# First feed-forward of a hybrid attention and recurrence step: a ring of its own for kept weight tiles, loaded one ahead

## Chip, cores and metric

One Trainium2 chip, one core. The metric is the device time of the kernel in microseconds: the median of three runs before the change is 1487.94 us (1484.69, 1487.94 and 1488.04). One further execution was profiled; every row below is from that one.

## What is computed

Two layers of a denoising step on 640 tokens (512 latent, 128 context) of width 1024. Layer 0 is attention, layer 1 a gated linear recurrence, and each is followed by a SwiGLU feed-forward of inner width 2816. Every sub-layer is normalised, scaled and shifted by columns that come from a small "adaLN" product, and added back through a gate. Cut to what the change touches:

```python
def _adaln(cond, w_mod, b_mod):
    m = jax.nn.silu(cond) @ w_mod + b_mod
    return jnp.split(m, N_MOD, axis=-1)

def _swiglu(x, w_gu, w_down):
    gate, up = jnp.split(x @ w_gu, 2, axis=-1)
    return (jax.nn.silu(gate) * up) @ w_down

# in the loop over the two layers
        f_c = _swiglu(_modulate(ctx, norm_g[i, 1], sh2_c, sc2_c), ffn_w_gu[i], ffn_w_down[i])
        f_l = _swiglu(_modulate(lat, norm_g[i, 1], sh2_l, sc2_l), ffn_w_gu[i], ffn_w_down[i])
        ctx = ctx + g2_c[:, None, :] * f_c
        lat = lat + g2_l[:, None, :] * f_l
```

## The kernel before

Every fp32 product is made of three matmuls on fp32r operands: an operand is split into a high part (a cast on ACT) and a low part (operand minus high part, on DVE), and PE adds high x high, high x low and low x high (lines 252 to 254, called by `chunk`). Tokens are the moving side in two halves of 320 columns. A *chunk* is 24 matmuls (8 slices of the inner dimension, three each) into one PSUM bank; chunks use three banks `mm` and two banks `mx` in turn, so PE may run some chunks ahead of the engines that read them.

The stage of interest is the first feed-forward (`ffn`, about 370 to 838 us of the profile). It works through the inner width in three blocks of 8, 7 and 7 tiles of 128. For each tile `j` of a block there are four chunks: two of the gate and two of the up product (the half of columns 320 to 640 goes first). Their banks are read by DVE (line 916 for the gate into `sg`, 924 for up into `up`, 927 for the product into `sg`), ACT copies a bias (238), applies SiLU (918), casts the hidden tile's high part (`big`, 1529), and DVE makes its low part (`big`, 1530). When all tiles of a block are done, the down projection of the block starts (`project`): 8 output tiles of two chunks, whose inner dimension is the block's hidden tiles. So the last slices of its first chunks are the hidden tile that was finished last. I call the two moments at which PE goes over from the up product of the last tile to the first chunk of the down projection the **handovers**: handover 1 at 476.82 us (block 0, 8 tiles) and handover 2 at 633.06 us (block 1, 7 tiles).

Three kinds of side work run in the gaps of this stage:

- The weight tiles of the stage itself: SP loads `raw`, ACT casts `whi` or `whx`, DVE makes `wlo` or `wlx`.
- adaLN columns (`mod_cols`, lines 283 to 292): POOL loads a 512 KB tile `mraw`, DVE reads it twice (`mprod`, line 291).
- Kept tiles (`keep`, lines 205 to 220): 33 weight tiles of later stages (`wi`, `wg`, `wlo`, `gu`) are split ahead of time and written back to DRAM. POOL loads a tile into `mraw`, ACT casts `kwh` from it (217), DVE writes `kwl` (218), and POOL stores both (220). The calls stand behind tiles of the feed-forward: two behind each of the last four tiles of block 0, one behind each output tile of its down projection, then about one per tile.

Before, kept tiles and adaLN tiles share one ring `mraw` of three buffers; `kwh` and `kwl` have one buffer each. The order of the instructions on each engine is set when the program is built, by a scheduler that moves work of `ffn` around within the limits of rings and dependences; each engine then runs its list in order. A POOL load waits in POOL's list until its buffer is free, and everything behind it in that list waits too. The weight loads of the stage are on SP's list, apart from these.

Of the kernel before, what the change touches and what calls it, by code (L numbers as in the profile page):

```python
# [9 lines left out]
F32 = mybir.dt.float32  # L10
F32R = mybir.dt.float32r
AF = mybir.ActivationFunctionType
ALU = mybir.AluOpType
AX = mybir.AxisListType

P = 128
D = 1024
KT = D // P
# [119 lines left out]
class _Step:  # L138
# [65 lines left out]

    def keep(self, todo, n):
        nc = self.nc
        for _ in range(min(n, len(todo))):
            name, f = key = todo.pop(0)
            raw = self.t([P, D], F32, "mraw", 3, self.sb)
            if name == "wg":  # L210
                nc.gpsimd.dma_start(raw.rearrange("p (f m) -> p f m", f=2), self.i[name][2 * f:2 * f + 2].rearrange("f p w d m -> p f (w d m)"))
            else:
                nc.gpsimd.dma_start(raw.rearrange("p (k m) -> p k m", k=KT), self.i[name][1, f] if name == "gu" else self.i[name][f])
            self.kept[key] = d = self.dram.tile([P, 2 * D], F32, tag=f"k{name}{f}", name=f"k{name}{f}")
            high, low = [self.t([P, D], F32R, n, 1, self.sb) for n in ("kwh", "kwl")]
            with self.tc.issue_after(self.mark[0]), self.tc.issue_after(self.mark[1]):
                nc.scalar.copy(high, raw)
                nc.vector.tensor_tensor(low, raw, high.bitcast(F32), ALU.subtract)
            for h, w in enumerate((high, low)):
                nc.gpsimd.dma_start(d[:, h * D:h * D + D], w.bitcast(F32))  # L220

    def two(self, src, x):
# [940 lines left out]
    def s_sums(self, q):  # L1163
        nc, g = self.nc, q["g"]
        q["u"], src = self.t([P, KT, P], F32, "raw", 3), q["u"]
        nc.sync.dma_start(q["u"], src)
        ss = q["S"] = [self.t([P, KT, P], F32, "sum", 2, self.sb) for _ in range(2)]
        s1, s2, s3, s4 = [s[:, a:a + KH] for s in ss for a in (0, KH)]
        g1, g2, u1, u2 = [t[:, a:a + KH] for t in (g, q["u"]) for a in (0, KH)]
        ops = (s1, u1, u2, ALU.add), (s2, s1, g1, ALU.subtract), (s3, g1, u1, ALU.subtract), (s4, g2, s2, ALU.subtract)  # L1170

        def run(two):
            def go(vector):
                for o in two:
                    (nc.vector if vector else nc.gpsimd).tensor_tensor(*o)
            return go
        return run(ops[:2]), run(ops[2:])
# [7 lines left out]
    def sum_weights(self, q, first=False):  # L1185
        for run, after in zip(self.s_sums(q), (self.pw, self.next)):
            with self.tc.issue_after(after):
                run(False)
        with self.tc.issue_after(self.last) if first else nullcontext():
            for i in range(2):  # L1190
                self.s_split(q, i)
# [360 lines left out]
    def run(self):  # L1552
        nc, tc, i, o = self.nc, self.tc, self.i, self.o
# [21 lines left out]
        with ExitStack() as banks:  # L1575
# [27 lines left out]
            for p in range(8):  # L1603
# [8 lines left out]
                if p == 6:  # L1612
# [5 lines left out]
                    for k in range(4):  # L1618
                        with tc.issue_after(self.evac) if k < 2 else tc.issue_after(self.low1), tc.issue_after(self.exp) if k > 1 else nullcontext(), tc.issue_after(self.cast) if k > 1 else nullcontext():
                            high, low = self.split(ohi[:, k], olo[:, k], O[:, k])  # L1620
# [5 lines left out]
            nc.sync.dma_start(o["nv"], V[:, 4])  # L1626
        xhi = self.big(n=NTOK + 2)
        xlo = self.big(n=NTOK + 2)
        self.nraw = 3
        self.new_x(xpool)  # L1630
        self.load_x(i["x"])
        xd = dram.tile([D, NTOK], F32, tag="xd", name="xd")
# [47 lines left out]
```

## Time and profile before

| what | value |
|---|---|
| median of three runs | 1487.94 us |
| the profiled execution, its own time | 1490.48 us |
| its span | 1488.7 us |
| PE busy | 1471.1 us, 99% |
| DVE busy | 1076.5 us, 72% |
| ACT busy | 728.4 us, 49% |
| POOL busy | 247.8 us, 17% |
| DMA moved | 255.35 MB, mean 172 GB/s |

PE is busy nearly all the time, so its share says little. What can be read is how fast matmuls start: a stretch in which fewer of them start than in an undisturbed one of equal length is a stretch in which PE lost time. Busy shares of DVE and ACT are means over stages; in the first feed-forward DVE is far above its mean.

### The profile page before, as it was taken

What the parts mean: (1) busy time and instruction counts of PE and PEld (TensorE: products, weight loads), DVE (VectorE), ACT (ScalarE), POOL (GpSimd) and SP (SyncE); (2) the same over time, 40 slices, a digit from 0 to 9 for tenths busy, and PEclk for the clock granted to TensorE, in tenths of its full rate; (3) what the DMA queues carried; (4) which work ended last, traced back from release to release, by engine and by line L of the source; (5) the groups of instructions that cost most, each with busy time, mean ns of one, the idle gap of its engine ahead of it and who ended that gap; (6) DMA issues with size and microseconds to landing.
All of it is one profiled execution on the core that took longest, in us unless ns stands there. A gap on an engine that the chain in (4) does not pass through costs nothing.

```text
span 1488.7 us, 26375 instructions
## 1 busy us (share of the span) xinstructions
PE 1471.1 (99%) x10379; PEld 1440.3 (97%) x10379; DVE 1076.5 (72%) x2054; ACT 728.4 (49%) x1345; POOL 247.8 (17%) x325
## 2 busy tenths in 40 slices
PE   8999999999999999999999999999999999999997
PEld 5999999899999999999999999999999999999997
DVE  6788887876678779887876479985866656655555
ACT  5666666754333234322434298864634343424244
POOL 0001000000012222211210001112132322222311
PEclk9999999999999999999999999999999999999999
DMA  9545554443369899876863744267242131313121
GB/s 371 183 149 172 170 157 146 125 157 100 114 185 313 303 357 321 306 246 223 308 228 123 253 145 142 85 233 243 87 132 85 57 114 57 114 57 104 56 69 71
DMA packets 84938, 255.35 MB, mean 172 GB/s; under 512 B 8992, under 2 KB 22480, under 8 KB 84688
## 3 DMA queue, kind: packets, MB, share of 16 engines
q1 hardware_dynamic: 58064, 157.06, 32.4%
q0 software_dynamic: 26576, 96.49, 19.1%
q8 instruction: 81, 1.33, 0.4%
q14 instruction: 41, 0.34, 0.1%
q10 hardware_dynamic: 176, 0.13, 0.0%
HBM read 206.18 MB, written 43.53 MB: 168 GB/s over the span
## 4 chain that ended last, share of the span: by engine, by line
PE 78%; DMA 8%; DVE 6%; ACT 4%; issue 3%; POOL 1%; DVEq 0%; ACTq 0%; POOLq 0%
PE mm L254 11%; PE mm L253 11%; PE mm L252 11%; PE mx L252 4%; PE mx L254 4%; PE mx L253 4%; PE mx L1203 3%; PE mx L1204 3%; PE mx L1205 3%; PE op L888 2%; DMA kwi<-kwh 2%; PE gp L1412 2%; DMA mraw<-in_wm 2%; PE tp L806 2%; DMA raw<-in_dn 1%
## 5 line engine op out<-in xcount | busy, mean ns | idle before, releaser
L252 PE MATMUL mm<-big,whi 128*128 128x320 f32 (+3 forms) x1010 | 311.0, 311 | 2.6 <-ACT big L1529 2.2
L253 PE MATMUL mm<-big,whi 128*128 128x320 f32 (+3 forms) x1010 | 312.8, 310 | 0.4 <-DVE big L1530 0.3
L254 PE MATMUL mm<-big,wlo 128*128 128x320 f32 (+3 forms) x1010 | 312.1, 310 | 0.0
L291 DVE SCALAR_TENSOR_TENSOR mprod<-mraw,csb 128x1024 f32<-128x1024 f32 x160 | 195.0, 1219 | 20.5 <-DMA mraw<-in_wm 20.2
L252 PEld LDWEIGHTS mm<-big,whi 128*128 128x128 f32 x1010 | 189.6, 189 | 4.7 <-ACT big L1529 2.8
L253 PEld LDWEIGHTS mm<-big,whi 128*128 128x128 f32 x1010 | 190.5, 189 | 2.0 <-DVE big L1530 0.9
L254 PEld LDWEIGHTS mm<-big,wlo 128*128 128x128 f32 x1010 | 190.1, 188 | 1.0
L1529 ACT CAST whi<-raw 128x1024 fp32r<-128x1024 f32 (+2 forms) x103 | 105.4, 1024 | 147.5 <-PE mm L253 91.6
L1530 DVE TENSOR_TENSOR wlo<-raw,whi 128x1024 fp32r<-128x1024 f32 (+2 forms) x103 | 127.1, 1235 | 33.3 <-ACT whi L1529 33.0
L253 PE MATMUL mm<-big,whx 128*128 128x320 f32 (+3 forms) x443 | 137.4, 310 | 0.0
L254 PE MATMUL mm<-big,wlx 128*128 128x320 f32 (+3 forms) x443 | 137.2, 310 | 0.0
L252 PE MATMUL mm<-big,whx 128*128 128x320 f32 (+3 forms) x443 | 137.0, 310 | 0.0
L595 DVE SCALAR_TENSOR_TENSOR x<-mm,G,x 128x320 f32<-128x320 f32 (+3 forms) x202 | 81.3, 436 | 54.6 <-PE mm L254 49.2
L252 PE MATMUL mx<-big,whi 128*128 128x320 f32 (+3 forms) x318 | 99.9, 315 | 0.0
L254 PE MATMUL mx<-big,wlo 128*128 128x320 f32 (+3 forms) x318 | 99.3, 312 | 0.0
L253 PE MATMUL mx<-big,whi 128*128 128x320 f32 (+3 forms) x318 | 99.2, 312 | 0.1
L287 POOL DMA_DIRECT2D mraw<-in_wm x80 | 42.7, 534 | 314.9 <-DVE mprod L291 209.8
L254 PEld LDWEIGHTS mm<-big,wlx 128*128 128x128 f32 x443 | 83.6, 189 | 0.0
L253 PEld LDWEIGHTS mm<-big,whx 128*128 128x128 f32 x443 | 83.5, 189 | 0.0
L252 PEld LDWEIGHTS mm<-big,whx 128*128 128x128 f32 x443 | 83.4, 188 | 0.0
L1530 DVE TENSOR_TENSOR wlx<-sum,whx 128x1024 fp32r<-128x1024 f32 x40 | 50.8, 1270 | 41.2 <-ACT whx L1529 41.2
L254 PE MATMUL mx<-big,wlx 128*128 128x320 f32 (+3 forms) x229 | 70.9, 310 | 0.0
(396 smaller groups left out, 3850.1 us busy)
## 6 DMA issues: line engine op xcount, KB each, us to landing
raw<-in_gu SPq DMA_DIRECT2D x84, 512.0 KB, 3.6
mraw<-in_wm POOLq DMA_DIRECT2D x80, 512.0 KB, 5.4
raw<-in_dn SPq DMA_DIRECT2D x24, 512.0 KB, 3.6
sw<-in_wm SPq DMA_DIRECT2D x16, 512.0 KB, 10.0
raw<-in_wqk SPq DMA_DIRECT2D x16, 512.0 KB, 4.5
mraw<-in_wi POOLq DMA_DIRECT2D x16, 512.0 KB, 6.6
kwi<-kwh POOLq DMA_DIRECT2D x16, 512.0 KB, 6.4
kwi<-kwl POOLq DMA_DIRECT2D x16, 512.0 KB, 6.1
```

The source lines that it names most:

```text
L252: nc.tensor.matmul(ps, hi[:, k], xhi[:, k, s], start=(k == 0), stop=False)
L253: nc.tensor.matmul(ps, hi[:, k], xlo[:, k, s], start=False, stop=False)
L254: nc.tensor.matmul(ps, lo[:, k], xhi[:, k, s], start=False, stop=(k == nk - 1))
L287: nc.gpsimd.dma_start(w, self.i["wm"][l * 6 + j - 2, f])
L291: nc.vector.scalar_tensor_tensor(prod, w, 1.0, self.csb[:, s], ALU.mult, ALU.mult, accum_out=out[:, s, f:f + 1])
L595: last = self.nc.vector.scalar_tensor_tensor(xs, ps[:, a - t0:b - t0], G[:, s, f:f + 1], xs, ALU.mult, ALU.add).ins
L806: turn = nc.tensor.transpose(tp[:, j * P:j * P + P], s[:, j * P:j * P + P], self.ident)
L1203: nc.tensor.matmul(ps, hi[:, k], xh[:, k], start=start and k == 0, stop=False, skip_group_check=not start)
L1204: nc.tensor.matmul(ps, hi[:, k], xl[:, k], start=False, stop=False, skip_group_check=not start)
L1205: nc.tensor.matmul(ps, lo[:, k], xh[:, k], start=False, stop=(k == KH - 1), skip_group_check=not start)
L1529: high = self.nc.scalar.copy(hi, v).ins
L1530: return high, self.nc.vector.tensor_tensor(lo, v, hi.bitcast(F32), ALU.subtract).ins
```

## The change

- Kept tiles get a ring `kraw` of two buffers in the pool of the stage. A call of `keep` no longer loads the tile that it splits: it takes the one loaded by the call before (the first call of all loads its own as well) and first asks for the load of the next tile on the list.
- The low part is written in place: DVE subtracts `kwh` from `kraw` and leaves the result in `kraw`, which is stored from there. The buffer `kwl` is gone. A buffer of `kraw` is thus free again when the store of the low part has landed, where a buffer of `mraw` was free when DVE had read it.
- The ring `mraw` of this stage has two buffers and holds adaLN tiles only.

Buffer space is the same: five tiles of 512 KB before (three `mraw`, `kwh`, `kwl`) and five after (two `mraw`, two `kraw`, `kwh`). The numbers of loads, casts, subtractions and stores are the same too.

```diff
     def keep(self, todo, n):
         nc = self.nc
+
+        def load():
+            if todo:
+                name, f = todo[0]
+                raw = self.t([P, D], F32R, "kraw", 2, self.sb)
+                v = raw.bitcast(F32)
...
+                    nc.gpsimd.dma_start(v.rearrange("p (k m) -> p k m", k=KT), self.i[name][1, f] if name == "gu" else self.i[name][f])
+                self.kraw = raw
+
         for _ in range(min(n, len(todo))):
+            if len(self.kept) == 0:
+                load()
             name, f = key = todo.pop(0)
-            raw = self.t([P, D], F32, "mraw", 3, self.sb)
...
+            raw = self.kraw
+            load()
             self.kept[key] = d = self.dram.tile([P, 2 * D], F32, tag=f"k{name}{f}", name=f"k{name}{f}")
-            high, low = [self.t([P, D], F32R, n, 1, self.sb) for n in ("kwh", "kwl")]
+            high = self.t([P, D], F32R, "kwh", 1, self.sb)
             with self.tc.issue_after(self.mark[0]), self.tc.issue_after(self.mark[1]):
-                nc.scalar.copy(high, raw)
-                nc.vector.tensor_tensor(low, raw, high.bitcast(F32), ALU.subtract)
-            for h, w in enumerate((high, low)):
+                nc.scalar.copy(high, raw.bitcast(F32))
+                nc.vector.tensor_tensor(raw, raw.bitcast(F32), high.bitcast(F32), ALU.subtract)
+            for h, w in enumerate((high, raw)):
                 nc.gpsimd.dma_start(d[:, h * D:h * D + D], w.bitcast(F32))
...
-        self.nraw = 3
+        self.nraw = 2
```

The scheduler builds another order from this. SP's list is the same, row for row. Lines behind `keep` have numbers that are 11 higher in the changed kernel.

On POOL, in the last tiles of block 1 (from some 13 us ahead of handover 2). Before, the load of a kept tile stands behind the low store of the tile before it (here `kwlo_7247`), and is followed by that tile's own stores:

```order
L220 DMA kwlo_7247<-kwh_7248 128x1024
L287 DMA mraw_7393<-in_wm 128x1024
L220 DMA kwlo_7247<-kwl_7249 128x1024
L213 DMA mraw_7399<-in_wlo 128x1024
L287 DMA mraw_7541<-in_wm 128x1024
L220 DMA kwlo_7401<-kwh_7402 128x1024
L220 DMA kwlo_7401<-kwl_7403 128x1024
```

After, at the same place, the same two kept tiles are `kwlo_7228` and `kwlo_7381`:

```order
L231 DMA kwlo_7071<-kraw_6916 128x1024
L231 DMA kwlo_7228<-kwh_7229 128x1024
L298 DMA mraw_7373<-in_wm 128x1024
L216 DMA kraw_7226<-in_wlo 128x1024
L231 DMA kwlo_7228<-kraw_7069 128x1024
L298 DMA mraw_7520<-in_wm 128x1024
L216 DMA kraw_7379<-in_wlo 128x1024
L231 DMA kwlo_7381<-kwh_7382 128x1024
L231 DMA kwlo_7381<-kraw_7226 128x1024
```

The load of a tile (`kraw_7226`) has moved ahead of the low store of the tile before it, and the load of the next one (`kraw_7379`) ahead of this tile's stores.

On ACT, at handover 1, from the last gate chunk of block 0 on. `big_4647` is the high part of the hidden tiles of the block, `sg` its last tile; before:

```order
L918 ACTIVATE sg_5741<-sg_5741,bias_5739 128x320
L217 CAST kwh_5702<-mraw_5699 128x1024
L238 COPY bias_5803<-mx_5778 128x2
L1529 CAST whx_6099<-raw_6097 128x1024
L1529 CAST big_4647<-sg_5741 128x320 x2
```

and after:

```order
L929 ACTIVATE sg_5737<-sg_5737,bias_5735 128x320
L249 COPY bias_5799<-mx_5774 128x2
L1540 CAST big_4647<-sg_5737 128x320
L228 CAST kwh_5699<-kraw_5688 128x1024
L1540 CAST whx_6090<-raw_6088 128x1024
L1540 CAST big_4647<-sg_5737 128x320
```

The first half of the hidden tile (columns 320 to 640) is now cast ahead of the kept tile, the second half behind it and behind a weight cast. DVE follows the same pattern: low part of the first half, the kept tile, `up`, `wlx`, `sg`, low part of the second half.

On PE, at handover 1, the first two chunks of the down projection, around their 28th matmul (`mx` is the first chunk, `mm` the second; `big_4648` is the low part). Before, the last slice of the first chunk stands in the middle of the second, twice cut apart:

```order
L254 MATMUL mm_5904<-big_4647,wlo_5874 128x320
L252 MATMUL mm_5904<-big_4647,whi_5873 128x320
L253 MATMUL mm_5904<-big_4648,whi_5873 128x320
L252 MATMUL mx_5877<-big_4647,whi_5873 128x320
L254 MATMUL mm_5904<-big_4647,wlo_5874 128x320
L252 MATMUL mm_5904<-big_4647,whi_5873 128x320
```

After, the first chunk is whole (24 matmuls in a row), and it is the last slice of the second chunk that is cut, with matmuls of the next output tile (`whx_5940`) between:

```order
L265 MATMUL mm_5898<-big_4647,wlo_5868 128x320
L263 MATMUL mm_5944<-big_4647,whx_5940 128x320
L263 MATMUL mm_5898<-big_4647,whi_5867 128x320
L264 MATMUL mm_5944<-big_4648,whx_5940 128x320
L265 MATMUL mm_5944<-big_4647,wlx_5941 128x320
```

Counted from the first matmul of the projection, the last slice of the first chunk now begins at matmul 21 (before: 29), and that of the second chunk at matmul 46. At handover 2 PE's list is the same before and after.

## Rows read from the trace of the kernel before

**Rows 1.** The page, busy time of each engine (us, share, instructions).

```profile
PE 1471.1 (99%) x10379; PEld 1440.3 (97%) x10379; DVE 1076.5 (72%) x2054; ACT 728.4 (49%) x1345; POOL 247.8 (17%) x325
```

**Rows 2.** Busy time by stretch: us, busy (instructions) by engine, PE clock, DMA share, GB/s.

```profile
633.00:651.00 18.00, 16.06 (x97) 15.57 (x96) 17.33 (x33) 4.97 (x8) 3.24 (x7) 0.91 0.73 249
...
653.00:671.00 18.00, 18.00 (x124) 18.00 (x123) 14.50 (x26) 4.13 (x5) 3.17 (x6) 1.00 0.80 264
```

**Rows 3.** Timeline of PE at handover 2: start, duration, instruction, wait before it.

```profile
635.57 0.30 PE L254 MATMUL mm<-big,wlo 128*128 128x320 f32 x1
637.70 0.41 PE L252 MATMUL mm<-big,whi 128*128 128x320 f32 x1 [1.83 <-ACT big L1529]
...
641.08 0.47 PE L252 MATMUL mx<-big,whi 128*128 128x320 f32 x1
```

**Rows 4.** Timeline of ACT, last tiles of block 1.

```profile
618.89 1.05 ACT L217 CAST kwh<-mraw 128x1024 fp32r<-128x1024 f32 x1 [0.33 <-DMA mraw<-in_wlo]
...
627.71 0.46 ACT L1529 CAST big<-sg 128x320 fp32r<-128x320 f32 x1 [2.49 <-DVE sg L927]
631.18 1.05 ACT L217 CAST kwh<-mraw 128x1024 fp32r<-128x1024 f32 x1 [3.01 <-DMA mraw<-in_wlo]
...
637.19 0.46 ACT L1529 CAST big<-sg 128x320 fp32r<-128x320 f32 x1 [1.50 <-DVE sg L927]
```

**Rows 5.** Timeline of DVE, last tiles of block 1.

```profile
611.76 1.23 DVE L291 SCALAR_TENSOR_TENSOR mprod<-mraw,csb 128x1024 f32<-128x1024 f32 x1 [1.32 <-DMA mraw<-in_wm]
...
632.27 1.23 DVE L218 TENSOR_TENSOR kwl<-mraw,kwh 128x1024 fp32r<-128x1024 f32 x1 [2.25 <-ACT kwh L217]
...
637.68 0.49 DVE L1530 TENSOR_TENSOR big<-sg,big 128x320 fp32r<-128x320 f32 x1 [0.52 <-ACT big L1529]
```

**Rows 6.** Timeline of POOL, the issues around that kept tile.

```profile
620.23 0.54 POOL L220 DMA_DIRECT2D kwlo<-kwh  x1 [3.33 <-ACT kwh L217]
...
622.83 0.54 POOL L220 DMA_DIRECT2D kwlo<-kwl  x1 [0.61 <-DVE kwl L218]
623.36 0.53 POOL L213 DMA_DIRECT2D mraw<-in_wlo  x1
```

**Rows 7.** Waits of ACT, 430 to 800 us: us in total, times, longest.

```profile
ACT kwh L217 <- DMA kwi<-kwh: 36.4, 8, 6.9
```

**Rows 8.** Timeline of PE: the first matmul of the down projection of block 0.

```profile
476.82 0.31 PE L252 MATMUL mx<-big,whi 128*128 128x320 f32 x1
```

**Rows 9.** Timeline of ACT at handover 1.

```profile
476.96 1.05 ACT L217 CAST kwh<-mraw 128x1024 fp32r<-128x1024 f32 x1 [1.14 <-DMA kwi<-kwh]
...
480.38 0.46 ACT L1529 CAST big<-sg 128x320 fp32r<-128x320 f32 x1 [1.37 <-DVE sg L927]
```

**Rows 10.** Timeline of DVE at handover 1.

```profile
480.27 0.48 DVE L924 TENSOR_TENSOR up<-mm,r 128x320 f32<-128x320 f32 x1
480.79 0.55 DVE L927 SCALAR_TENSOR_TENSOR sg<-up,bias,sg 128x320 f32<-128x320 f32 x1
481.25 1.22 DVE L1530 TENSOR_TENSOR wlx<-raw,whx 128x1024 fp32r<-128x1024 f32 x1
482.39 0.89 DVE L1530 TENSOR_TENSOR big<-sg,big 128x320 fp32r<-128x320 f32 x2
```

**Rows 11.** Timeline of POOL: the low store of the first kept tile.

```profile
439.71 0.53 POOL L220 DMA_DIRECT2D kwi<-kwl  x1 [1.84 <-DVE kwl L218]
```

**Rows 12.** Chain of waits, 436 to 480 us, transfers of POOL's queue: start, us.

```profile
440.23 6.35 DMA mraw<-in_wm
...
455.96 6.25 DMA mraw<-in_wm
...
465.38 5.92 DMA mraw<-in_wi
...
472.70 4.16 DMA kwi<-kwh
```

**Rows 13.** All instructions of the tile kwh: its transfers, shortest, median, longest.

```profile
DMA to landing us min/median/max: 2.9/5.5/9.6
```

More of the change, by code (lines that the diff above doesn't have):

```diff
@@ L206, in keep @@
         nc = self.nc
+        def load():
[3 more added lines that the diff above has]
+                v = raw.bitcast(F32)
+                if name == "wg":
+                    nc.gpsimd.dma_start(v.rearrange("p (f m) -> p f m", f=2), self.i[name][2 * f:2 * f + 2].rearrange("f p w d m -> p f (w d m)"))
+                else:
+                    nc.gpsimd.dma_start(v.rearrange("p (k m) -> p k m", k=KT), self.i[name][1, f] if name == "gu" else self.i[name][f])
+                self.kraw = raw
         for _ in range(min(n, len(todo))):
+            if len(self.kept) == 0:
+                load()
             name, f = key = todo.pop(0)
-            raw = self.t([P, D], F32, "mraw", 3, self.sb)
[L210 to L213, printed above, removed]
+            raw = self.kraw
+            load()
             self.kept[key] = d = self.dram.tile([P, 2 * D], F32, tag=f"k{name}{f}", name=f"k{name}{f}")
-            high, low = [self.t([P, D], F32R, n, 1, self.sb) for n in ("kwh", "kwl")]
+            high = self.t([P, D], F32R, "kwh", 1, self.sb)
             with self.tc.issue_after(self.mark[0]), self.tc.issue_after(self.mark[1]):
-                nc.scalar.copy(high, raw)
-                nc.vector.tensor_tensor(low, raw, high.bitcast(F32), ALU.subtract)
-            for h, w in enumerate((high, low)):
+                nc.scalar.copy(high, raw.bitcast(F32))
+                nc.vector.tensor_tensor(raw, raw.bitcast(F32), high.bitcast(F32), ALU.subtract)
+            for h, w in enumerate((high, raw)):
                 nc.gpsimd.dma_start(d[:, h * D:h * D + D], w.bitcast(F32))
```

## The prediction

> **What bounds the kernel now.** I read the engine line of the page first: PE is busy for 99% of the span [rows 1]. So work taken off another engine gives nothing by itself. The change can only give back, or add, time in which PE stands still or runs slowly inside the first feed-forward, and the first question is how much of that there is. The second view is therefore the busy time by stretch, read for the number of matmuls and the granted clock. In an undisturbed stretch of 18 us PE has 124 matmuls, one per 0.145 us. In the 18 us around handover 2 it has 97 [rows 2]. The missing 27 are worth 27 x 0.145 = 3.9 us. In the rest of the stage no place is short by more than 0.3 us. So the whole stage has some 4 us to give back, 0.27% of the time.
>
> The third view, PE's own timeline, splits the 3.9 us. After the matmul at 635.57 the next one begins at 637.70, with 1.83 us of waiting for the high part of the last hidden tile [rows 3]. Then the clock falls: the mean granted clock of the stretch is 0.91 where the later one has 1.00, and at 641.08 a matmul takes 0.47 instead of 0.30 us, at the lower of the two levels, 1.2 GHz [rows 2, 3]. So a pause of about 2 us costs as much again in slow matmuls (3.9 - 1.83 = 2.1 us).
>
> The fourth view, the timelines of ACT, DVE and POOL, says why the hidden tile was late. The cast at 637.19 waited for DVE [rows 4]. DVE had stood still for 2.25 us until 632.27, because its next instruction, the low part of a kept tile, waited for the cast of that tile on ACT [rows 5]. ACT had been free since 627.71 + 0.46 = 628.17 and stood in front of that cast for 3.01 us until the load of the tile had landed [rows 4]. POOL had issued this load at 623.36, right behind the low store of the tile before it [rows 6]. It took 7.8 us. That chain is what the change cuts into.
>
> **Part by part.** *The number of operations does not change*: 33 loads, casts, subtractions and 66 stores, as many adaLN tiles. No term.
>
> *Loading one ahead, at handover 2.* In the new order the load of a kept tile goes out behind the high store of the tile before it, and that tile in turn was loaded a whole tile earlier, so its cast need not wait for a load as at 618.89 [rows 4]. What still bounds the cast of the tile before is the one buffer `kwh`: the previous high store must have landed. Casts are one per tile here (96 matmuls x 0.145 = 13.9 us), against a cast of 1.05, an issue of 0.54 and a store of 5.5 us at the median [rows 4, 6, 13], so that buffer is free in time. If that cast comes at any time up to where it now is (618.89), its store and one adaLN load go out and the next load is issued by 622 at the latest, 1.4 us earlier than now; if the cast comes where the new order allows it, right behind the first bias of its tile, some 8 us earlier. With the 7.8 us of the old load it lands between 622 and 630. ACT comes to it at 628.17. So ACT's wait of 3.01 goes to between 0 and 1.6, DVE's 2.25 to between 0 and 0.9. PE needs the tile 18 matmuls into the projection, at 633.06 + 2.6 = 635.7, and had it 2.0 us later. With 2.25 us less on DVE, PE does not wait; with only 1.35 us less it waits 0.65. I take the end without a wait, since DVE also had other waits for loads of this ring on the way (1.32 us at 611.76 [rows 5]) that move the same way. Term: -3.9 us, with -2.0 as the other end.
>
> *What is late next at handover 2?* Low parts, 0.5 us behind the high ones [rows 5]; inside the margin.
>
> *Low part in place.* A `kraw` buffer is held from the issue of its load until its low store has landed. One round is a load, a cast (1.05), a subtraction (1.23), a store and two issues of 0.54: with 5.7 us for each transfer (the mean of the four in [rows 12]) that is 5.7 + 1.05 + 1.23 + 5.7 + 1.1 = 14.8 us for two tiles in two buffers. Where two kept tiles fall on 13.9 us (last tiles of block 0 and its down projection) the ring is just about the bound, and POOL, ACT and DVE wait for it. From block 1 on, with one tile per 13.9 us, it is not. A lag of DVE of some us costs PE nothing by itself, as five banks of 3.5 us lie between; in the trace ACT waits 36.4 us for the store of `kwh` in eight places, and PE waits for none of them [rows 7]. It costs only at a handover. This is handover 1.
>
> *Handover 1, first half.* Without the old interleaving PE needs the last slice of the first chunk at matmul 21, at 476.82 + 21 x 0.145 = 479.9 [rows 8]. In the trace its cast began at 480.38 and its low part, the first of the two in one row, at 482.39 [rows 9, 10]. Left there, PE would wait some 2.5 us. But in the new order the cast stands right behind the bias of its chunk, ahead of the kept tile (which held that bias up by its wait of 1.14 and its 1.05 [rows 9]) and of the weight cast, and its low part right behind: 2.2 us earlier for the high part, at 478.2, and the low part 0.5 us after it instead of 2.0. Taken as covered, margin 1 us.
>
> *Handover 1, second half.* Here the kept tile now stands ahead. PE needs the high part at matmul 46, 476.82 + 6.7 = 483.5. From the start of the kept cast it takes 1.05 (cast) + 1.23 (in place) + 0.48 (`up`) + 1.22 (`wlx`) + 0.55 (`sg`) + 0.46 (hidden cast) = 5.0 us [rows 5, 9, 10], so that cast must begin by 478.5. What it waits for is a series of five transfers in one of the two buffers, from the first low store on (439.71 [rows 11]): store, load, cast, subtraction, store, load, cast, subtraction, and then the load that stands behind that on POOL. With t for a transfer: 439.7 + 5t + 2 x (1.05 + 1.23) + 5 x 0.54 = 447.0 + 5t. At 5.7 it is 475.5, 3.0 us of margin; the margin is gone at t = 6.3. The four measured in this stretch run from 4.16 to 6.35 [rows 12], the longest anywhere to 9.6 [rows 13]. Taken at 0, with the 0.3 us of the old wait gone or not.
>
> *adaLN ring of two.* Two tiles fall on 13.9 us; with two buffers a load has that round less the reading (twice 1.23 [rows 5]), against a landing of some 6.3 us [rows 12]. Covered by about 5 us, and a DVE wait of that size is free between handovers. Below nothing it can't go, above it is part of the handover risk.
>
> *A rule that speaks against the change.* In the trace POOL's list stands in front of an issue until what it waits for is there (3.33 us in front of the store at 620.23) and the two behind it go out later [rows 6]. The Trainium skill says the same in general (DMA: Bandwidth & Descriptors, Anatomy of one DMA — SWDGE (gpsimd) path): the engines that move data never wait for a semaphore, the issuing sequencer does so before dispatch. By that rule every load that now waits for a store to land also holds up the stores and adaLN loads behind it; this is the third rival below. The same section gives about 2.0 us plus bytes / 436 GB/s per transfer, 3.2 us for 512 KB as an estimate; by that the series would end at 463, well ahead of its time, and the ring could never be late. The four transfers in [rows 12] took 4.2 to 6.4, and the measured ones decide.
>
> **Sum.** -3.9 at handover 2, 0 at handover 1: the profiled execution would go from 1490.48 to 1486.6. The median of the runs is 2.5 us below the profiled time; the same step from it gives 1487.94 - 3.9 = 1484.0. One of the three runs is at 1484.69 already, so the wait may be missing in some runs, which speaks against more than 3.9.
>
> **Rivals.**
> 1. *Only part comes back.* The load is early by 1.4 us alone, or DVE is held by something else: -2.0, or 0 if the change doesn't bring the load ahead at all on the chip. For it: the static order moves the load past one store only. Time 1486 to 1488.
> 2. *The wait moves to handover 1 and is small.* Five transfers at 6.3 to 6.7: PE waits up to 1.8 us there, and at 2 us the clock falls as at handover 2. Net between -3.9 and 0: 1484 to 1488. Break-even is 1.8 + 2.1 = 3.9, at t = 6.7.
> 3. *Slower: the queue of POOL decides handover 1.* Loads that wait for landed stores hold up the high stores behind them, and the series runs at t = 7.5 (between the 6.35 and the 9.6 of the rows): the cast begins at 484.5, PE waits 6.0 us and loses 2.1 more to the clock, less 3.9: +4.2, so 1492.1. Against it: no transfer of that stretch took 7 us, and the bytes moved stay the same.
> 4. *More than forecast*: less lag of DVE frees something not seen as a wait; the stage shows no more than 0.3 us besides. Below 1483.5.
>
> **How the numbers follow.** Forecast (both handovers free) 0.55; rival 1 0.17; rival 2 0.13; rival 3 0.08; rival 4 0.07. A difference of 0.3% (4.5 us) is about what a measurement can tell from none. The forecast is 0.26% and so inside it, near the edge: of its 0.55 I put 0.2 below 1483.5, as the three runs lie 3.4 us apart. With rival 4 that makes 0.27 for faster. Slower by over 4.5 us needs t above 7.5: 0.07 with some room for what I don't see. The rest, 0.66, is within. The range leaves out 0.1 on each side: down to 1482.0 (forecast with 2 us of scatter), up to 1489.0 (rivals 1 and 2 whole, rival 3 not).
>
> **What would show it.** In the profile of the changed kernel: 18 us around handover 2 with some 124 matmuls and clock 1.00; no wait of ACT for `kraw` there, and DVE's wait in front of the kept tile below 0.9; at handover 1 no wait of PE, the kept cast begun before 478.5, and the hidden low part of the first half written before 480. POOL waiting for landed stores between 440 and 540. I am wrong if PE waits at 480 to 485, or still at 635, or if PE shows a pause of 2 us at a place where it had none.

## The result, and the profile after

The changed kernel takes 1495.98 us (median of nine runs, 1492.02 to 1502.95) where the kernel before takes 1486.63 (nine runs, 1484.69 to 1490.93). The ratio is 1.006, with an interval of 1.0045 to 1.0075: slower by some 9 us. The forecast was 1484.0, in a range that ended at 1489.0. It was wrong in sign.

Both profiled executions are unusual ones: that of before (1490.48 us) is one of its longest runs, that of after (1492.02) the shortest of its nine. So the two pages lie much closer together than the kernels do. PE is as busy as in [rows 1]:

```profile
PE 1472.5 (99%) x10379; PEld 1441.4 (97%) x10379; DVE 1078.9 (72%) x2054; ACT 727.4 (49%) x1345; POOL 247.2 (17%) x325
```

The busy time by stretch of after, as in [rows 2]: most of the stage, 22 us ahead of the pause at handover 2, and the two stretches shown before.

```profile
430.00:840.00 410.00, 407.40 (x2747) 406.65 (x2746) 322.51 (x566) 142.81 (x250) 77.44 (x144) 1.00 0.78 264
616.00:638.00 22.00, 22.00 (x150) 21.74 (x148) 21.04 (x35) 10.12 (x21) 5.85 (x11) 1.00 0.89 310
633.00:651.00 18.00, 16.43 (x99) 15.94 (x99) 15.23 (x27) 6.10 (x12) 4.26 (x8) 0.91 0.97 333
653.00:671.00 18.00, 18.00 (x123) 18.00 (x123) 13.46 (x26) 2.67 (x3) 3.07 (x6) 1.00 0.75 248
```

Handover 2 still has 99 matmuls and a clock of 0.91 (97 and 0.91 before). PE's timeline of after, as in [rows 3], shows that pause, and a new one at handover 1:

```profile
485.95 0.42 PE L263 MATMUL mm<-big,whi 128*128 128x320 f32 x1 [1.03 <-ACT big L1540]
...
639.46 0.41 PE L263 MATMUL mm<-big,whi 128*128 128x320 f32 x1 [1.46 <-ACT big L1540]
639.98 0.41 PE L264 MATMUL mm<-big,whi 128*128 128x320 f32 x1
...
641.11 0.47 PE L263 MATMUL mx<-big,whi 128*128 128x320 f32 x1
```

*Handover 1.* The first half came out as forecast: its low part is written by 479.99 (the first row, DVE of after), and PE, which begins the projection at 477.99 in this run and needs it 21 matmuls later, at 481.0, doesn't wait for it. The kept cast ahead of the second half (the second row, ACT, as in [rows 9]) begins at 481.10, not ahead of 478.5 (479.7 when counted from the later start of this run), and it waits for its load.

```profile
479.50 0.49 DVE L1541 TENSOR_TENSOR big<-sg,big 128x320 fp32r<-128x320 f32 x1 [0.52 <-ACT big L1540]
...
481.10 1.05 ACT L228 CAST kwh<-kraw 128x1024 fp32r<-128x1024 f32 x1 [1.64 <-DMA kraw<-in_wi]
```

POOL of after says where the time went on the way. A load of a kept tile stands in front of the queue until the low store of the tile two before it has landed (the first two rows name such waits), and what stands behind the load waits with it: the low store in the third row goes out at 458.56, though DVE had written its data by 456.9. The last row is the load that the cast at 481.10 waits for:

```profile
444.67 0.74 POOL L214 DMA_DIRECT2D kraw<-in_wg  x1 [1.71 <-DMA kwi<-kraw]
...
458.03 0.53 POOL L216 DMA_DIRECT2D kraw<-in_wi  x1 [1.54 <-DMA kwi<-kraw]
458.56 0.53 POOL L231 DMA_DIRECT2D kwg<-kraw  x1
...
475.29 0.53 POOL L216 DMA_DIRECT2D kraw<-in_wi  x1
```

*Handover 2.* DVE of after, as in [rows 5], and ACT's cast of the same kept tile. The wait of 2.25 us right ahead of the handover is gone: the low part at 633.42 follows its predecessor directly. But 26 us earlier DVE stood 5.03 us, for a kept tile again, and then had hardly a gap to make it up: it is busy 21.04 of the 22 us from 616 to 638. That this earlier wait is what reaches PE is read from the trace here; e9 and e10 below test it.

```profile
607.26 1.23 DVE L229 TENSOR_TENSOR kraw<-kraw,kwh 128x1024 fp32r<-128x1024 f32 x1 [5.03 <-ACT kwh L228]
...
632.18 1.05 ACT L228 CAST kwh<-kraw 128x1024 fp32r<-128x1024 f32 x1 [0.73 <-DMA kraw<-in_wlo]
...
633.42 1.23 DVE L229 TENSOR_TENSOR kraw<-kraw,kwh 128x1024 fp32r<-128x1024 f32 x1
```

### The profile page after: what moved, and what is told of

Same layout as the page of the kernel before. It is cut to its first block, busy times and chain, and to the rows that moved or that the text cites. A ratio compares the mean times of both kernels' runs of the same rounds, so it can differ in the third digit from the quotient of the medians.

```text
span 1489.7 us, 26374 instructions
## 1 busy us (share of the span) xinstructions
PE 1472.5 (99%) x10379; PEld 1441.4 (97%) x10379; DVE 1078.9 (72%) x2054; ACT 727.4 (49%) x1345; POOL 247.2 (17%) x325
## 4 chain that ended last, share of the span: by engine, by line
PE 77%; DMA 8%; DVE 6%; ACT 3%; issue 3%; POOL 2%; DVEq 0%; ACTq 0%; SPq 0%; POOLq 0%
PE mm L264 11%; PE mm L265 11%; PE mm L263 11%; PE mx L263 4%; PE mx L264 4%; PE mx L265 4%; DMA kraw<-in_wi 3%; PE mx L1214 3%; PE mx L1215 3%; PE mx L1216 3%; PE op L899 2%; PE tp L817 2%; PE gp L1423 2%; DMA kwi<-kraw 1%; PE mc L1215 1%
## 5 line engine op out<-in xcount | busy, mean ns | idle before, releaser
L228 ACT CAST kwh<-kraw 128x1024 fp32r<-128x1024 f32 x33 | 34.6, 1049 | 88.7 <-DMA kraw<-in_wi 42.4
```

The lines of the kernel that those rows point to most:

```text
L228: nc.scalar.copy(high, raw.bitcast(F32))
```

## The experiments

**The theories.** After's own trace suggests three. *A*: a buffer of the kept ring goes through load, cast, subtraction, store and landing; with two buffers that round is slower than the calls for kept tiles (one per 6.95 us in the second half of block 0 and its down projection). The tiles fall behind, ACT and DVE stand in front of them in their lists, and PE pauses where their lag comes through. *B*: the adaLN ring of two holds up POOL's list, and with it the kept tiles. *C*: the fault is the order that the scheduler builds.

The place of the load in the program changes nothing. With the load written in its own call, not one tile ahead, the program builds the same lists of instructions on all engines, row for row. So "one ahead" does nothing by itself; what changes are the rings, and the order that the scheduler builds for them.

The table sums up all kernels. "Missing" is the number of matmuls that a kernel lacks in the stretch from 430 to 840 us of its profiled run, against the 2782 of the kernels without a pause; "lost" is that times 410 / 2782 = 0.147 us. "One per" is the mean distance of kept casts on ACT, from the third to the sixteenth. Each ratio is to the runs of before that were taken along with the kernel's own, so it isn't quite the quotient of two medians of the table. The medians are of 6 to 12 runs, that of e8 of two.

| kernel | median us | ratio to before, interval | profiled us | missing | lost us | one per us |
|---|---|---|---|---|---|---|
| before | 1486.63 | | 1490.48 | 30 | 4.4 | 8.2 |
| before, again | one run | | 1486.27 | 9 | 1.3 | 8.1 |
| after | 1495.98 | 1.0060, 1.0045 to 1.0075 | 1492.02 | 35 | 5.2 | 8.7 |
| after, again | one run | | 1496.89 | 67 | 9.9 | 9.0 |
| e1 scratch halved | 1496.97 | 1.0065, 1.0047 to 1.0083 | 1498.25 | 82 | 12.1 | 8.9 |
| e2 kept ring 3 | 1486.63 | 0.9998, 0.9987 to 1.0010 | 1485.84 | 0 | 0 | 8.0 |
| e3 adaLN ring 3 | 1490.56 | 1.0021, 1.0011 to 1.0031 | 1492.47 | 47 | 6.9 | 9.1 |
| e4 low part apart | 1485.71 | 0.9990, 0.9980 to 1.0000 | 1485.37 | 0 | 0 | 8.3 |
| e6 even calls | 1486.54 | 0.9996, 0.9986 to 1.0005 | 1487.67 | 0 | 0 | 11.9 |
| e7 in place, shared ring | 1487.81 | 1.0006, 0.9993 to 1.0019 | 1488.16 | 10 | 1.5 | 8.2 |
| e8 kept ring 1 | 1505.15 | 1.0121, 1.0088 to 1.0154 | 1500.39 | 92 | 13.6 | 13.0 |
| e9 block 1 light | 1495.38 | 1.0062, 1.0050 to 1.0075 | 1492.24 | 54 | 8.0 | 8.6 |
| e10 block 0 even | 1486.35 | 0.9996, 0.9988 to 1.0005 | 1485.43 | 0 | 0 | 10.7 |
| e11 before, even | 1485.73 | 0.9991, 0.9979 to 1.0003 | 1485.73 | 0 | 0 | 11.9 |

The profiled time less the lost time lies between 1484.2 and 1487.7 in every row; the runs of a kernel without a pause lie as far apart (e10: 1484.81 to 1488.51). So the difference between these kernels is, as closely as the runs can tell, in pauses of PE in this stage (with the slow matmuls behind them).

No kernel with the calls of the change brings its tiles as fast as they are called for. Those with no pause or short ones (before, e2, e4, e7) bring one per 8.0 to 8.3 us, those that are clearly slower one per 8.6 to 9.1; e8, with one buffer, is a case apart.

### Room for a sixth buffer, and a second profile of after: e1_scratch, e12_after_again

```diff
-                prod = self.t([P, D], F32, "mprod", 1, self.sb)
+                prod = self.t([P, D], mybir.dt.bfloat16, "mprod", 1, self.sb)
```

> The changed kernel with one edit: the scratch product of the adaLN reading (its values are read by nobody, only its running sum) is half as wide, which frees 2 KB per partition for the next three kernels. The instruction lists are the same, row for row. Every theory expects the time of the changed kernel, 1493 to 1499 us, and 1.2 us for a reading as before. Its profile is a second look at the changed kernel, whose first one was of the shortest of its nine runs: PE should lose more than 5 us at the two handovers together, some 10 to 14.

> The changed kernel, unchanged: a look at a run of the usual length. Theory A: the cast of the kept tile ahead of the second half of handover 1 begins behind 478.5 us by as much as PE then pauses, with transfers of more than 6.3 us; pauses at both handovers, together with their slow matmuls 5 to 14 us; 1492 to 1500.

Both times came out as expected, 1496.97 and 1496.89 us, and e1 has its pauses at the two handovers. PE of e1 at handovers 1 and 2, then ACT at handover 1:

```profile
487.39 0.64 PE L263 MATMUL mm<-big,whi 128*128 128x320 f32 x1 [3.10 <-ACT big L1540]
...
644.83 0.63 PE L263 MATMUL mm<-big,whi 128*128 128x320 f32 x1 [3.82 <-ACT big L1540]
```

```profile
482.54 1.05 ACT L228 CAST kwh<-kraw 128x1024 fp32r<-128x1024 f32 x1 [2.98 <-DMA kraw<-in_wi]
```

At handover 2 the chain of waits of e1 ends on a weight load of SP's queue that took 9.07 us, so the last link there isn't the same in every run:

```profile
631.95 9.07 DMA raw<-in_dn
```

The second profile of after (e12) missed where the time goes. PE's waits at the handovers are 0.55 and 0.57 us, with no slow matmuls behind them, and the largest pause is where no theory had put it, in the middle of block 1. PE, DVE and ACT there:

```profile
615.14 0.64 PE L263 MATMUL mm<-big,whi 128*128 128x320 f32 x1 [4.39 <-DVE sg L927]
```

```profile
613.46 1.23 DVE L229 TENSOR_TENSOR kraw<-kraw,kwh 128x1024 fp32r<-128x1024 f32 x1 [5.32 <-ACT kwh L228]
```

```profile
612.38 1.04 ACT L228 CAST kwh<-kraw 128x1024 fp32r<-128x1024 f32 x1 [6.83 <-DMA kraw<-in_wi]
```

Read upwards: the load is late, ACT stands 6.83 us for it, DVE 5.32 us for ACT, and PE 4.39 us for DVE to read a bank: the lag has used up the banks that lie between.

### Which ring: e2_kept3, e3_adaln3, e4_low_apart

All three with the halved scratch of e1.

```diff
 e2
-                raw = self.t([P, D], F32R, "kraw", 2, self.sb)
+                raw = self.t([P, D], F32R, "kraw", 3, self.sb)
 e3
-        self.nraw = 2
+        self.nraw = 3
 e4
-            high = self.t([P, D], F32R, "kwh", 1, self.sb)
+            high, low = [self.t([P, D], F32R, n, b, self.sb) for n, b in (("kwh", 1), ("kwl", 1))]
...
-                nc.vector.tensor_tensor(raw, raw.bitcast(F32), high.bitcast(F32), ALU.subtract)
-            for h, w in enumerate((high, raw)):
+                nc.vector.tensor_tensor(low, raw.bitcast(F32), high.bitcast(F32), ALU.subtract)
+            for h, w in enumerate((high, low)):
```

> The changed kernel with a ring of three for kept tiles (room from the halved scratch). Theory A, the round of the kept ring (load, cast, subtraction, store until landed, in two buffers) is too long, and DVE, which has no slack there, reaches the handovers late: a third buffer takes a third off the round, PE waits at neither handover for more than 1 us, 1482 to 1488. Theory B, the adaLN ring of two holds up POOL's list and with it the kept tiles behind: the adaLN ring is still two, so 1492 to 1499. Theory C, neither ring but the order that the scheduler builds: this order is nearly the changed kernel's, 1492 to 1499.

> The changed kernel with a ring of three for adaLN tiles (same room), the kept ring two as in the change. Theory A: the kept ring is as slow as before, 1492 to 1499, and ACT still waits for loads of kept tiles ahead of both handovers. Theory B: the list of POOL runs free, 1482 to 1488. Theory C: order nearly the changed kernel's, 1492 to 1499.

> The changed kernel with the low part in a buffer of its own, as before the change (same room): a kept buffer is free when DVE has read it, not when its store has landed. Rings of two and two. Theory A: the store leaves the round, which falls from two transfers to one, 1482 to 1488. Theory B: the adaLN ring is still two, 1492 to 1499. Theory C: 1490 to 1499.

e2 and e4 came out as theory A has it: no matmul missing, and the time is that of the kernel before. The stretch of handover 2 in e4:

```profile
633.00:651.00 18.00, 18.00 (x123) 18.00 (x123) 16.05 (x27) 4.77 (x6) 4.81 (x9) 1.00 0.91 324
```

The rings of e4 are as small as in the change (two and two); the landing of the low store is out of the buffer's round, at the price of a sixth buffer. So, with these calls, the low part in place is what makes a ring of two too short. B falls as the whole cause, since e2 and e4 keep the adaLN ring of two and lose nothing.

Theory C doesn't fall as cleanly. SP's list is that of after, but for other rings the scheduler builds the other lists anew. Against after, e2's lists have 6 added or removed lines on PE, 38 on ACT, 68 on DVE and 46 on POOL; e4's have 8, 26, 56 and 72. At handover 1 both put the kept cast ahead of the bias and of both halves of the hidden tile, where it stood before the change. ACT there, first e2, then e4:

```profile
473.91 1.05 ACT L228 CAST kwh<-kraw 128x1024 fp32r<-128x1024 f32 x1 [2.50 <-DMA kwi<-kwh]
...
473.64 1.05 ACT L228 CAST kwh<-kraw 128x1024 fp32r<-128x1024 f32 x1 [0.88 <-DMA kwi<-kwh]
```

In that order a late tile would hold up more of the hidden tile, not less. But it isn't late: the cast begins 2.2 and 3.0 us ahead of the first matmul of the projection (476.10 and 476.63), where in after it begins 3.1 us behind it. So what the rings change is when the tile comes. How much of that is the round on the chip, and how much the order that is built for the rings, e2 and e4 can't separate. e9 below, which has the order of after, shows that the order alone makes no pause at handover 1.

e3 fits neither A nor B: it gives back 6 of the 10 us, though the kept tiles come no faster (one per 9.1 us) and both pauses are there, of 1.60 and 2.58 us, in a profile that is the longest of its twelve runs. So a third adaLN buffer takes part of the loss away. By which path isn't settled: DVE's list changes in it too, in 32 lines.

### In place alone: e7_low_shared4

The kernel before, with a shared ring of four and the low part in place.

```diff
-            raw = self.t([P, D], F32, "mraw", 3, self.sb)
+            raw = self.t([P, D], F32, "mraw", 4, self.sb)
-            high, low = [self.t([P, D], F32R, n, 1, self.sb) for n in ("kwh", "kwl")]
+            high, low = self.t([P, D], F32R, "kwh", 1, self.sb), raw.bitcast(F32R)
...
-        self.nraw = 3
+        self.nraw = 4
```

> The kernel before with the low part in place alone: kept and adaLN tiles share one ring, of four (the room of the separate low buffer goes to it), no load ahead. Per 13.9 us two kept tiles hold a buffer for some 17 us each (two transfers of 6 to 7, cast, subtraction, issues) and two adaLN tiles for some 9 to 10: 52 to 54 of the 55.6 that four buffers have. Theory A with rings that cannot lend to each other as the fault: 1485 to 1490. If the low part in place is the whole fault: 1492 to 1499.

1487.81 us, no measurable difference to before. The low part in place is not a fault in itself: in the same room, four buffers that both kinds of tile may use are enough, where two and two are not.

### How often the tiles are called for: e6_even, e10_block0_even, e9_block1_light, e11_before_even

```diff
-KEEP = ((0, 0, 0, 0, 2, 2, 2, 2), (2, 1, 1, 1, 1, 1, 0), (2, 1, 1, 1, 1, 1, 1))
-DOWN = ((1,) * KT, (0, 0, 0, 1, 1, 0, 0, 0))
 e6 and e11
+KEEP = ((2, 2, 2, 1, 1, 1, 1, 1), (1, 1, 1, 1, 1, 1, 1), (1, 1, 1, 1, 1, 1, 1))
+DOWN = ((0, 1, 0, 1, 0, 1, 0, 1), (0, 1, 0, 1, 0, 1, 0, 1))
 e10
+KEEP = ((1, 1, 1, 1, 1, 1, 1, 1), (2, 1, 1, 1, 1, 1, 0), (2, 1, 1, 1, 1, 1, 1))
 e9
+KEEP = ((0, 0, 0, 0, 2, 2, 2, 2), (0, 0, 0, 1, 1, 1, 0), (3, 2, 2, 2, 1, 1, 1))
```

> The changed kernel, rings as in the change, the same 33 kept tiles but called for evenly, about one per 13.9 us from the first tile of block 0 on, in place of none in its first four tiles and two per 13.9 us in the last four and their down projection. Theory A (two in-place buffers give one tile per 8 to 9 us, which is too slow for one per 7 and enough for one per 14): no pause of PE over 1 us at either handover, 1484 to 1488. Rival (transfers that run late near the handovers, or the order, whatever the demand): pauses stay, 1491 to 1499.

> The changed kernel, rings as in the change, with the eight kept tiles of block 0 spread over its eight tiles, one each; all else as in the change. Two in-place buffers give a tile per 8 to 9 us and are asked for one per 14 up to handover 1: no pause there (0 instead of 3 to 5 us). The down projection still asks for one per 7 us, so lag and a pause at handover 2 of up to 7 us with its slow matmuls: 1487 to 1493. A rival by which the ring's round does not matter expects both pauses, 1493 to 1499.

With the rings of the change, even calls take every pause away (e6). It is enough to spread the eight tiles of block 0 (e10): handover 2 is then free too, though the calls around it are as in the change. So the pause at handover 2 goes back to block 0 and its down projection. The lag stands in the lists already: the calls of block 1 are about one per 13.9 us in both, but ahead of handover 2 ACT has a kept cast per 9.4 us in after (594.7 to 632.2) and one per 12.8 in e10 (595.1 to 633.6). How much more is added as the lists run isn't separated. e10 came out below its expected range: the down projection alone builds up no lag that PE shows.

> The changed kernel, rings as in the change, with the four kept tiles of the first three tiles of block 1 called for in block 2 instead; block 0, its down projection and the last tiles ahead of handover 2 as in the change. If the pause at handover 2 is lag carried along (kept tiles that fell behind in block 0 and its down projection, and a DVE that has no gap to catch up in), it goes, and the pause at handover 1 stays with its 3 to 5 us: 1489 to 1492. If it is made on the spot (late loads of the last 14 us ahead of it), both pauses stay: 1493 to 1499.

e9 fits neither expectation. Its time, 1495.38 us, lies in the range for a pause made on the spot, but the pauses are elsewhere. Handover 2 is free, as lag has it. But the calls moved to block 2 are two per 13.9 us there, and now PE pauses at the next handover behind that place, where no kernel but e8 had a pause:

```profile
788.97 0.64 PE L263 MATMUL mx<-big,whi 128*128 128x320 f32 x1 [5.61 <-ACT big L1540]
```

The pause goes where the dense calls go. The second miss is handover 1, which has no pause in this run (the shortest of its six, 3 us below their median), though the lists are those of the changed kernel until well behind it, row for row. ACT shows why: the load landed in time.

```profile
476.78 1.05 ACT L228 CAST kwh<-kraw 128x1024 fp32r<-128x1024 f32 x1 [1.44 <-DMA kraw<-in_wi]
```

That makes four runs of one list, which test the bound of the prediction: the kept cast must begin 478.5 - 476.82 = 1.7 us behind the first matmul of the projection.

| run | first matmul | kept cast | behind the bound | wait of PE |
|---|---|---|---|---|
| e9 | 475.73 | 476.78 | -0.6 | none |
| after, again | 478.04 | 480.68 | 0.9 | 0.55 |
| after | 477.99 | 481.10 | 1.4 | 1.03 |
| e1 | 477.36 | 482.54 | 3.5 | 3.10 |

The bound holds to 0.4 us. What differs, in one and the same order, is when the tile comes.

> The kernel before, rings as before the change, with the even calls of the earlier experiment (33 kept tiles, about one per 13.9 us). If what the kernel before still loses at handover 2 is lag of the same kind, it goes: 1484 to 1487, the shortest of all by up to 2 us; if not, 1486 to 1489.

e11 has no pause, and at 1485.73 us can't be told from the kernel before. No version beat that measurably; its usual run has little to give back (next).

### A second profile of before: e5_before_again

> The kernel before, unchanged: a second look, since its first profile was of a long run (1490.48 us where the median of 29 is 1486.97). If the 3.9 us of handover 2 belong to every run, some 27 matmuls are missing there again in a run of the usual length. If they belong to that run, the time is 1485 to 1488 and fewer than 14 are missing, so that there was less than 2 us to give back in the median run.

1486.27 us, nine matmuls missing. PE at handover 2:

```profile
635.08 0.42 PE L252 MATMUL mm<-big,whi 128*128 128x320 f32 x1 [0.68 <-ACT big L1529]
```

The wait is 0.68 us and the clock doesn't fall (matmuls behind it take 0.31 us). So the 3.9 us that the prediction set out to win were those of a long run; this one, of the usual length, loses 1.3.

### One buffer: e8_kept1

```diff
-                raw = self.t([P, D], F32R, "kraw", 2, self.sb)
+                raw = self.t([P, D], F32R, "kraw", 1, self.sb)
...
-        self.nraw = 2
+        self.nraw = 3
```

> The changed kernel with one buffer for kept tiles and three for adaLN tiles (the same room). Theory A: a round of one buffer (load 6.7, cast 1.05, subtraction 1.23, store 5.8, issues 1.1) is 16 us for one tile; 16 tiles are called for at one per 7 us, so they fall behind by 9 us each, less what the banks and the list let through: slower by 60 to 160 us. Theory B (adaLN ring) and theory C (order): not slower than the changed kernel by more than 10.

Slower than before by 18 us (two runs, 1500.39 and 1509.91). That is 9 us more than after: within what B and C allowed, and far less than I had for A, so the time of this run speaks for none of them. The list shows where my estimate went wrong: with one buffer the scheduler itself sets the kept casts apart, they come every 13.0 us, and PE misses nothing until its one long pause, at 796.76 (10.54 us), in block 2, into which the tiles were pushed. The place of a call in the program only says from when on a tile may come; the list decides. That with two buffers it puts them closer than the chip delivers points to transfers that it takes for shorter than they are; that is argued, not shown.

e8 also shows transfers at a lower load of the DMA engines. Loads and low stores of kept tiles issued from 440 to 560 us (count, size, median us to landing), in e8:

```profile
kwi<-kraw POOLq DMA_DIRECT2D x8, 512.0 KB, 4.3
kraw<-in_wi POOLq DMA_DIRECT2D x8, 512.0 KB, 4.2
```

and in e1:

```profile
kwi<-kraw POOLq DMA_DIRECT2D x11, 512.0 KB, 6.9
...
kraw<-in_wi POOLq DMA_DIRECT2D x10, 512.0 KB, 6.6
```

The mean busy share of the DMA engines in that stretch is 0.77 in e8 and 0.90 in e1. These times run from the issue and hold it. The links of one buffer's round then add up to 4.2 + 4.3 + 1.05 + 1.23 = 10.8 us, against casts every 13.0; those of two buffers to 6.6 + 6.9 + 2.3 = 15.8 for two tiles, against 2 x 8.9 = 17.8. In both, some 2 us of a round are waiting between the links. The second buffer made the tiles come 1.5 times as fast, not twice; the transfers took 1.6 times as long.

## Why the prediction was wrong, step by step

- **The step that failed is *Low part in place*, and the series of handover 1 with it: both add up the links of a buffer's round and put the waits between the links at nothing.** The series can be checked link by link. In the trace the parts of the series, from the issue of the first low store to the start of the cast ahead of the second half, are these (us, the four runs of one list):

| part | forecast | e9 | after, again | after | e1 |
|---|---|---|---|---|---|
| five transfers with their issues | 31.2 | 29.3 | 30.1 | 30.8 | 31.7 |
| two casts and two subtractions | 4.6 | 4.6 | 4.6 | 4.6 | 4.6 |
| waits between the links | 0 | 4.2 | 5.0 | 4.8 | 6.0 |
| sum | 35.8 | 38.2 | 39.8 | 40.2 | 42.3 |

  The bound is at 478.5 - 439.7 = 38.8 on this scale (in every run PE begins the projection 37.1 us behind that store), and the forecast left 3.0 us to it. The transfers kept to what I had allowed. I took 5.7 us each and 0.54 for the issue; but the four of [rows 12] run from the issue and hold it, so it was counted twice, and that covers what they took, 6.2 in after (3.5 to 8.6). What uses up the margin are waits for things outside the series. In after the third kept tile has landed at 453.25, and its cast waits 1.4 us more, for the high store of the tile before it to leave the one buffer `kwh`:

```profile
454.61 1.05 ACT L228 CAST kwh<-kraw 128x1024 fp32r<-128x1024 f32 x1 [2.91 <-DMA kwi<-kwh]
```

  Then its low store stands 1.6 us in POOL's list behind the load at 458.03. That load waits for the low store of the other buffer, which was issued at 448.11 and took 9.6 us to land (DMA issues of after from 448.2 to 448.6 us):

```profile
kwi<-kraw POOLq DMA_DIRECT2D x1, 512.0 KB, 9.6
```

  The other 1.8 us are smaller gaps, none above 0.9. A better t would not have shown this. The median transfers of before from 440 to 560 us are

```profile
kwi<-kwl POOLq DMA_DIRECT2D x12, 512.0 KB, 5.8
...
mraw<-in_wi POOLq DMA_DIRECT2D x11, 512.0 KB, 6.9
```

  and with three loads of 6.9 and two low stores of 5.8 the series ends at 439.7 + 32.3 + 4.6 = 476.6, still ahead of the bound.
- **The round of the kept ring** had the same fault: 14.8 us for two tiles (13.7 with the issues counted once), "just about the bound" at 13.9, where two tiles take 17.4 to 18.0 (2 x 8.7 to 2 x 9.0). In after the links add up to 6.1 + 6.9 + 2.3 = 15.3 by the medians of the stretch (load, low store, cast and subtraction). The rest, 2 to 3 us, is waiting.
- **"A lag of DVE of some us costs PE nothing by itself"** was wrong, and it hid the larger part of the loss. Handover 1 by itself lost 1.2 us in after, 0.7 in e12 and 4.6 in e1 (8, 5 and 31 matmuls missing from 430 to 560 us). Behind it, where the lag reaches PE, after lost 3.5 us at handover 2, e1 6.6 there, and e12 7.5 in the middle of block 1, at no handover, and 1.0 at handover 2. With calls every 6.95 us both kernels fall behind, after by about 2 us a tile (8.7 to 9.0), before by 1.2 (8.1 to 8.2). That the banks cover the smaller lag and not the larger is the likely reading; no run shows where the limit lies.
- **Handover 2.** The local part was right: ACT's wait for the load fell from 3.01 to 0.73 us (its cast at 632.18), and DVE's wait went. The term of -3.9 failed all the same, and the pause stayed: DVE came late from 26 us earlier (5.03 us). I had taken the last wait ahead of the pause for its cause, and not asked whether DVE had any gap left to recover in.
- **The base.** -3.9 us were taken off the median, though they were read in one of the longest runs. I had written that the wait may be missing in some runs; it is nearly missing in the usual one.
- **adaLN ring of two.** DVE's wait for its loads fell from 18.2 to 1.3 us (430 to 660 us), and e2 and e4 lose nothing with it: covered, as forecast, as long as the kept tiles come in time. e3 says that it isn't free once they lag.
- **The rivals.** Rival 3 had the place, the sign and the mechanism (loads that wait for landed stores and hold up what is behind them), at a chance of 0.08. It put the loss into a t of 7.5, which no mean of the series reached, and a wait of 6.0 us at handover 1, where 0.55 to 3.10 were measured; and it stopped at 1492.1 because it let handover 2 go free. Rival 2 had the size of the wait in the profiled run of after (up to 1.8 us; 1.03), but handover 2 free as well. POOL of after waits 25.2 us, in eight places from 430 to 660 us, for low stores of the tiles `kwi` alone, with others queued behind. The Trainium skill (DMA: Bandwidth & Descriptors, Anatomy of one DMA — SWDGE (gpsimd) path) says that a wait for a semaphore happens on the issuing sequencer, before it dispatches. The trace agrees. The same section of the Trainium skill gives 3.2 us a transfer, an estimate from its fixed part and its rate. Of the medians of POOL's 512 KB transfers from 440 to 560 us only that of the `kwi` high stores of e8 is as short (3.0 us); in after the loads of `kwi` tiles take 6.1.
- **What would show it.** I had named a pause at 480 to 485 or one still at 635 as proof against me; both came, within a few us of these places, and so did POOL's waits for landed stores.

## What to carry to other kernels

Before a buffer is held longer (here until its store has landed), work out the buffer's round and set it against how often buffers are asked for. Take the transfers from the stretch in question, see whether their times hold the issue already, and add what each link waits for outside the round: here the one buffer `kwh`, and POOL's list behind a load that waits for a store. If the round loses, the lag adds up and can show far from its cause. Here DVE, busy for 21.04 of 22 us, did not make up a wait of 5 us in 26. And before a pause is priced, profile a second run: here the first was among the longest.

## What the runs showed of the hardware

- A 512 KB transfer of POOL's queue has no fixed time. From 440 to 560 us the median load of a `kwi` tile took 4.2 us in e8, at a DMA busy share of 0.77, and 6.1 to 6.9 in after, e1 and before, at 0.90 to 0.92. The share alone doesn't set it: in e11, at 0.77 too, it took 5.6. The rows of after and e11:

```profile
kraw<-in_wi POOLq DMA_DIRECT2D x10, 512.0 KB, 6.1
...
mraw<-in_wi POOLq DMA_DIRECT2D x8, 512.0 KB, 5.6
```

- PE's clock: behind waits of 0.55, 0.68, 1.03 and 1.60 us it stayed at the upper level, 2.4 GHz (granted clock 1.00 from 486 to 494 us in e3, behind 1.60). Behind 1.46 us in after, and behind 1.83 us and more elsewhere, matmuls ran at 0.47 us, the lower level, 1.2 GHz. The wait in one row doesn't sort them, since 1.60 left the clock up and 1.46 did not. In after the next matmul was late as well (it began 0.52 us behind the first, at 639.98), in e3 it began 0.26 us behind; whether that decides isn't shown. The rows of after stand above; those of PE in e3:

```profile
486.21 0.41 PE L263 MATMUL mm<-big,whi 128*128 128x320 f32 x1 [1.60 <-ACT big L1540]
486.47 0.30 PE L264 MATMUL mm<-big,whx 128*128 128x320 f32 x1
```
